# A hybrid decoder layer on one core: every SBUF tile at a new address, and a 1088-byte pitch between the token slices of x and merged

## The chip, the core and the metric

The kernel runs on one NeuronCore of one Trainium2 chip. The metric is the device time of one execution in microseconds (us). PE is TensorE, with its weight loads shown apart as PEld; DVE is VectorE, ACT is ScalarE, POOL is GpSimd and SP is SyncE, which here only issues DMAs. SBUF has 128 partitions; an address below is a byte address within each partition, the same one in all 128. PSUM takes the results of PE.

## The reference

One layer on 256 tokens of width 2048, in float32. The normalised input goes through one wide projection (12416 columns) that feeds two mixers, RWKV-7 time mixing ("a") and block-sparse attention ("b"); each result is gated, projected back to 2048 columns, the two are merged by sigmoid gates, and one output projection with a residual closes the layer:

```python
h = rms_norm(x, norm_w)
p = h @ w_in                                   # (256, 2048) @ (2048, 12416)
(p_r, p_k, p_v, z_a, p_wd, p_ad, p_q, p_kq, p_vq, z_b, g_a, g_b) = split(p)
y_a = rwkv7_mix(p_r, p_k, p_v, p_wd, p_ad, ...) * silu(z_a)      # (256, 1024)
y_b = moba_attention(p_q, p_kq, p_vq, ...) * silu(z_b)           # (256, 1024)
merged = sigmoid(g_a) * (y_a @ w_proj_rwkv) + sigmoid(g_b) * (y_b @ w_proj_moba)
out = x + merged @ w_out
```

## The kernel before

All large products run as three float32r matmuls: each operand is split into a high part and a low part (the rest), and high times high, high times low and low times high are added up in PSUM. Weights stream in from HBM in blocks of 1 MB: SP issues the load into one of two `raw` buffers, ACT writes the high part to one of three `hi` buffers (line 216), DVE writes the low part to one of three `lo` buffers (line 222). One such `hi` or `lo` tile is 128 partitions by 1024 numbers, 4096 bytes a partition.

There are two kinds of large product. `mm_fm` (line 329) keeps a 128x128 piece of the weights in PE and streams 256 tokens past it: the weights are the stationary operand, a slice of 256 tokens (1024 bytes a partition) is the moving one. `mm_tm` (lines 347 to 349) keeps 128 tokens in PE and streams 512 columns of the weights. The token operand comes from one of these tiles:

- `xh` and `xl`, the parts of x, with 16 slices of 256 tokens (one for each 128 rows of the weights, index k). Most of the input projection is `mm_fm` on them: k, r, v, the two silu gates and the two merge gates, 3504 matmuls; q, k and v of the attention are `mm_tm` on them, 576 matmuls.
- the parts of the gated mixer results, written by `y_split` into tiles that other uses have left free: `qn` (high) with `kn` (low), then `vq` with `v`, for y_b; the two halves of `bk`, then `BK` with a low part, for y_a. They hold four slices each. 768 `mm_fm` matmuls.
- `mgh` and `mgl`, the parts of merged, which take the place of `xh` and `xl` and are the stationary operand of the output projection: 336 `mm_tm` matmuls of 512 columns and 96 of 256 in the last block.

In `mm_fm` the three matmuls of one piece follow each other as high weights with high tokens, high weights with low tokens, low weights with high tokens; then come the next 128 columns, and after four of these the next k. The 128x128 pieces of a `hi` or `lo` tile are 512 bytes apart. The weights of each matmul are loaded by an instruction of their own (PEld) while the matmul before it runs.

The order of instructions on PE, ACT and DVE is fixed when the program is built, by the order in which `run_jobs` writes out loads, splits, matmuls and small pieces of the mixers' work. SBUF addresses are given by tile pools in the order in which tiles are first asked for: `T` (line 55) and `C` (line 64) ask for named tiles, and equal names share one place. Before the change, small tiles with sizes such as 396 or 4160 bytes stand among the large ones, so that large tiles begin at addresses such as 92416 or 217792.

Of the kernel before, what the change touches and what calls it, by code (L numbers as in the profile page):

```python
# [10 lines left out]
F32R = mybir.dt.float32r  # L11
# [6 lines left out]
P = 128  # L18
D = 2048
S = 256  # L20
KT = D // P
# [15 lines left out]
def tile_hybrid_block(ctx: ExitStack, tc: tile.TileContext, x, pv, wdu, wau,  # L37
                      w_in, w_pr, w_pm, w_out, out):
    nc = tc.nc
    act, dve, pool, pe, sp = nc.scalar, nc.vector, nc.gpsimd, nc.tensor, nc.sync  # L40

    cp = ctx.enter_context(tc.tile_pool(name="cp", bufs=1))
    wp = ctx.enter_context(tc.tile_pool(name="wp", bufs=2))
    sb = ctx.enter_context(tc.tile_pool(name="sb", bufs=1))
    dp = ctx.enter_context(tc.tile_pool(name="dp", bufs=1, space=bass.MemoryType.DRAM))
    pm = ctx.enter_context(tc.tile_pool(name="pm", bufs=4, space=bass.MemoryType.PSUM))
    psd = ctx.enter_context(tc.tile_pool(name="psd", bufs=4, space=bass.MemoryType.PSUM))

    cnt = [0]

    def nm(s):
        cnt[0] += 1
        return f"{s}_{cnt[0]}"

    def T(tag, shape, dt=F32, bufs=1):
        return sb.tile(shape, dt, tag=tag, name=nm(tag), bufs=bufs)

    def PSM():
        return pm.tile([P, 512], F32, tag="pm", name=nm("pm"))
# [2 lines left out]
        return psd.tile([P, 512], F32, tag="ps", name=nm("ps"))  # L62

    def C(name, shape, dt=F32):
        return cp.tile(shape, dt, tag=name, name=name)

    def f32(ap):
        return ap.bitcast(F32)


    xs = [[T(t, [P, 1024]) for t in row] for row in (("k", "cs"), ("a", "kk"))]

    def load_x(c0, c1):
# [3 lines left out]

    load_x(0, 512)
    epsr = C("epsr", [P, 1])
    pool.memset(epsr, RMS_EPS)  # L80
    ident = C("ident", [P, P])
    make_identity(nc, ident)
    PV = C("pv", [P, PV_N])
    pool.dma_start(PV, pv)
    warm = C("warm", [P, 1])
# [3 lines left out]
    m2 = C("m2", [P, 2, 64], U8)  # L89
    mq = C("mq", [P, 2, P], U8)  # L90
    mtmp = T("LL1", [P, 3, P])
    mone = T("sg", [P, P])
    pool.memset(mone, 1.0)
    for i, (step, op) in enumerate(((1, ALU.is_gt), (1, ALU.is_ge), (-1, ALU.is_ge))):
# [25 lines left out]
    X64 = T("X64", [P, 16, 64])  # L120
# [1 line left out]
        pool.memset(ap, 0.0)  # L122


    xh = C("xh", [P, KT, S], F32R)
    xl = C("xl", [P, KT, S], F32R)
    ssx = C("ssx", [P, 2, 2])
    rsx = C("rsx", [P, 2])
    rbc = C("rbc", [P, S])
# [39 lines left out]
    def normed(o, ps):  # L169
        dve.tensor_tensor(o.rearrange("p (f t) -> p f t", f=2), ps.rearrange("p (f t) -> p f t", f=2),  # L170
                          rbc2, ALU.mult)
# [186 lines left out]
    wa = C("wa", [P, S])  # L358
    xx = C("xx", [P, 4, S], F32R)
# [249 lines left out]
    yaT = C("yaT", [P, 8, S])  # L609
# [150 lines left out]
    oT = C("oT", [P, 8, S])  # L760
# [145 lines left out]
    def gate_post(key, i):  # L906
        def post(st):
            if not gates:
                for tag, n in (("LL0", 4), ("LL1", 4), ("X64", 2), ("UV", 4), ("a", 2)):
                    gt = T(tag, [P, n, 512])  # L910
                    gslots.extend(gt[:, u, :] for u in range(n))
            for j in range(2):
                gt = gslots.pop(0)
                normed(gt, st["ps"][j])
                act.activation(gt, gt, AF.Sigmoid)
                gates[key, 2 * i + j] = gt
        return post
# [15 lines left out]

    def y_split(key, src):
        for i in range(2):
            tags = ((("qn", "kn"), ("vq", "v")), (("bk",), ("BK", "ep")))["ba".index(key)][i]
            if len(tags) == 1:
                yy = T(tags[0], [P, 2, 4, S], F32R)
                yh, yl = yy[:, 0], yy[:, 1]
            else:  # L940
                yh, yl = T(tags[0], [P, 4, S], F32R), T(tags[1], [P, 4, S], F32R)
            ysp.setdefault((key, "h"), []).append(yh)
            ysp.setdefault((key, "l"), []).append(yl)
            y = src[:, 4 * i:4 * i + 4, :].rearrange("p f t -> p (f t)")
            zs = zsil[key, i].rearrange("p a t -> p (a t)")
            hv, lv = yh.rearrange("p f t -> p (f t)"), yl.rearrange("p f t -> p (f t)")
            dve.tensor_tensor(y, y, zs, ALU.mult)
            act.activation(hv, y, AF.Copy)
            yield
            dve.tensor_tensor(lv, y, f32(hv), ALU.subtract)  # L950
            yield
# [16 lines left out]
    mh_t, ml_t = [], []  # L968

    def pa_post(i):  # L970
        def post(st):
            if not mh_t:
                mh_t.append(cp.tile([P, KT, S], F32R, tag="xh", name="mgh"))
                ml_t.append(cp.tile([P, KT, S], F32R, tag="xl", name="mgl"))
            mt = T(("cs", "kk")[i % 2], [P, 2, 512])
            for j in range(2):
                m = mt[:, j, :]
                dve.tensor_tensor(m, gates["a", 2 * i + j], st["ps"][j], ALU.mult)
                dve.tensor_tensor(m, m, mrg[i, j], ALU.add)
                f0 = 4 * i + 2 * j  # L980
                hv = mh_t[0][:, f0:f0 + 2, :].rearrange("p f t -> p (f t)")
                lv = ml_t[0][:, f0:f0 + 2, :].rearrange("p f t -> p (f t)")
                act.activation(hv, m, AF.Copy)
                dve.tensor_tensor(lv, m, f32(hv), ALU.subtract)
        return post
# [54 lines left out]
    for i in range(2):  # L1040
        post = z_post("a", i, ("qkn", "lora")[i])
        if i == 1:
            post = then(post, (y_split("b", oT), None), (y_split("a", yaT), "y"))
        chunk(w_in, C_ZA + 512 * i, 512, KT, fm_x, post)
# [56 lines left out]
```

## Time and profile before

| | |
|---|---|
| time before, median of 3 runs | 836.4 us (835.27 to 838.43) |
| the profiled execution's own time | 836.63 us |
| its span, first to last instruction | 834.9 us |
| granted TensorE clock over the span | 0.998 of full speed |
| PE busy | 821.7 us, 98% of the span |
| DVE busy, ACT busy | 550.3 us (66%), 423.4 us (51%) |

The span is what the trace shows; the profiled execution's time is 1.7 us longer, and 0.2 us over the median. A busy PE is not yet a PE at its best: the recorded durations of matmuls overlap, so that the time from one start to the next is less than a duration, and it is that spacing that adds up to the span.

### The profile page before, as it was taken

The numbers are of one execution on the slowest core, as the hardware profiler recorded it, in microseconds if no ns is written. First come the engines' busy times: TensorE is split into PE (matmuls) and PEld (weight loads), VectorE is DVE, ScalarE is ACT, GpSimd is POOL, SyncE is SP. The second block draws the span as 40 slices with busy tenths as digits, with TensorE's granted clock in tenths as the row PEclk, the third lists the DMA queues.
The fourth block names the chain that finished last, engine by engine and source line by source line (L and its number), as shares of the span: only waits on it lengthen the run. The fifth ranks groups of instructions, "written<-read, shape, count | busy, mean of one in ns | idle before, by whom it ended". The sixth has DMA issues, their size and how long they took to land.

```text
span 834.9 us, 15904 instructions
## 1 busy us (share of the span) xinstructions
PE 821.7 (98%) x6770; PEld 763.3 (91%) x6770; DVE 550.3 (66%) x776; ACT 423.4 (51%) x568; POOL 28.9 (3%) x42
## 2 busy tenths in 40 slices
PE   8999999999999999999989999999999999999998
PEld 8999878899998788899989998899999999998887
DVE  5769958956569649769955578644554566665553
ACT  6785435544437576445434467654444444443332
POOL 5001200000000002000000000000000000000000
PEclk9999999999999999999999999999999999999999
DMA  8564555664434444455673324566555555556772
GB/s 305 179 199 153 178 163 165 201 177 153 150 108 142 158 152 152 156 173 187 200 220 105 106 98 151 177 202 198 186 184 193 201 186 169 201 176 203 249 231 99
DMA packets 83207, 145.78 MB, mean 175 GB/s; under 512 B 11568, under 2 KB 13872, under 8 KB 83136
## 3 DMA queue, kind: packets, MB, share of 16 engines
q1 hardware_dynamic: 71584, 138.55, 51.2%
q10 hardware_dynamic: 11520, 6.16, 2.7%
q8 instruction: 53, 0.87, 0.4%
q14 instruction: 18, 0.15, 0.1%
q0 software_dynamic: 32, 0.05, 0.0%
HBM read 141.61 MB, written 3.15 MB: 173 GB/s over the span
## 4 chain that ended last, share of the span: by engine, by line
PE 92%; ACT 3%; DVE 2%; DMA 2%; issue 1%; SPq 0%; ACTq 0%; DVEq 0%
PE pm L329 56%; PE pm L348 9%; PE pm L347 9%; PE pm L349 9%; PE ps L534 1%; PE ps L672 1%; PE ps L679 1%; ACT bk L849 1%; PE ps L878 1%; DMA td<-kk 1%; DMA cs<-td 1%; PE ps L831 1%; PE ps L696 1%; DVE lo L222 1%; ACT hi L216 1%
## 5 line engine op out<-in xcount | busy, mean ns | idle before, releaser
L222 DVE TENSOR_TENSOR lo<-raw,hi 128x1024 fp32r<-128x1024 f32 (+1 forms) x259 | 316.3, 1225 | 212.9 <-ACT hi L216 212.0
L216 ACT ACTIVATE hi<-raw 128x1024 fp32r<-128x1024 f32 (+1 forms) x259 | 272.6, 1055 | 339.1 <-PE pm L329 193.1
L329 PE MATMUL pm<-xh,hi 128*128 128x256 f32 x1168 | 326.8, 282 | 0.4 <-ACT xh L144 0.4
L329 PE MATMUL pm<-xl,hi 128*128 128x256 f32 x1168 | 324.9, 280 | 0.0
L329 PE MATMUL pm<-xh,lo 128*128 128x256 f32 x1168 | 323.9, 280 | 1.0 <-DVE lo L222 1.0
L329 PEld LDWEIGHTS pm<-xh,hi 128*128 128x128 f32 x1168 | 220.4, 190 | 3.2 <-issue 0.8
L329 PEld LDWEIGHTS pm<-xh,lo 128*128 128x128 f32 x1168 | 220.0, 190 | 2.6 <-DVE lo L222 1.4
L329 PEld LDWEIGHTS pm<-xl,hi 128*128 128x128 f32 x1168 | 220.8, 190 | 1.0 <-issue 0.3
L348 PE MATMUL pm<-lo,xh 128*128 128x512 f32 x192 | 76.3, 397 | 0.0
L349 PE MATMUL pm<-hi,xl 128*128 128x512 f32 x192 | 75.5, 393 | 0.0
L347 PE MATMUL pm<-hi,xh 128*128 128x512 f32 x192 | 74.1, 401 | 0.0
L348 PE MATMUL pm<-lo,mgh 128*128 128x512 f32 (+1 forms) x128 | 48.4, 378 | 0.0
L349 PE MATMUL pm<-hi,mgl 128*128 128x512 f32 (+1 forms) x128 | 48.0, 376 | 0.0
L347 PE MATMUL pm<-hi,mgh 128*128 128x512 f32 (+1 forms) x128 | 44.4, 377 | 0.0
L349 PEld LDWEIGHTS pm<-hi,xl 128*128 128x128 f32 x192 | 36.1, 188 | 7.8 <-issue 0.2
L348 PEld LDWEIGHTS pm<-lo,xh 128*128 128x128 f32 x192 | 36.1, 188 | 7.7 <-DVE lo L222 0.6
L347 PEld LDWEIGHTS pm<-hi,xh 128*128 128x128 f32 x192 | 35.9, 188 | 7.8 <-issue 0.5
L347 PEld LDWEIGHTS pm<-hi,mgh 128*128 128x128 f32 x128 | 24.0, 188 | 4.7
L349 PEld LDWEIGHTS pm<-hi,mgl 128*128 128x128 f32 x128 | 24.0, 188 | 4.7
L348 PEld LDWEIGHTS pm<-lo,mgh 128*128 128x128 f32 x128 | 24.0, 188 | 4.4
L566 DVE TENSOR_TENSOR tmp<-sg,kk 64x31 f32<-64x31 f32 (+15 forms) x62 | 20.6, 331 | 4.6 <-DMA sg<-gd 3.5
L329 PE MATMUL pm<-bk,hi 128*128 128x256 f32 x128 | 22.8, 281 | 0.0
(275 smaller groups left out, 990.6 us busy)
## 6 DMA issues: line engine op xcount, KB each, us to landing
raw<-in_w_in_dram SPq DMA_DIRECT2D x94, 1024.0 KB, 5.0
raw<-in_w_out_dram SPq DMA_DIRECT2D x16, 1024.0 KB, 5.6
raw<-in_w_proj_moba_dram SPq DMA_DIRECT2D x8, 1024.0 KB, 5.1
raw<-in_w_proj_rwkv_dram SPq DMA_DIRECT2D x8, 1024.0 KB, 5.2
raw<-in_w_in_dram SPq DMA_DIRECT2D x5, 512.0 KB, 6.4
k<-in_x_dram ACTq DMA_DIRECT2D x4, 256.0 KB, 5.3
r<-in_x_dram ACTq DMA_DIRECT2D x4, 256.0 KB, 4.6
k<-in_x_dram SPq DMA_DIRECT2D x2, 256.0 KB, 4.8
```

What stands on the lines that cost most here:

```text
L216: act.activation(job["hi"][:, c], job["src"][:, c], AF.Copy)
L222: dve.tensor_tensor(job["lo"][:, c], job["src"][:, c], f32(job["hi"][:, c]), ALU.subtract)
L329: pe.matmul(o, (hi, hi, lo)[ps][:, i, cs], (mh, ml, mh)[ps](k), start=(k == 0 and fi % 2 == 0 and ps == 0), stop=(k == jb["last"] and ps = ...
L347: pe.matmul(o, sh[:, k, ts], hi[:, i, cs], start=(k == 0), stop=False)
L348: pe.matmul(o, sh[:, k, ts], lo[:, i, cs], start=False, stop=False)
L349: pe.matmul(o, sl[:, k, ts], hi[:, i, cs], start=False, stop=end)
L534: pe.matmul(pss[p][:, c * P:(c + 1) * P], bk[sl, fi, c].rearrange("p a t -> p (a t)"), ar[sl, fi, c].rearrange("p a t -> p (a t)"), start= ...
L566: dve.tensor_tensor(tv, gcol.to_broadcast([64, nt, j + 1]), trow.to_broadcast([64, nt, j + 1]), ALU.mult)
L672: pe.matmul(ps[64 * p:64 * p + 64, c0 + 64 * fi:c0 + 64 * fi + 64], LL[p][:, fi, c, which, :], UV[:, c, p, fi, :], start=(fi == 0), stop=( ...
L679: pe.matmul(ps[sl, c0 + 64 * fi:c0 + 64 * fi + 64], ar[sl, fi, c, which, :], St[sl, fi, :], start=False, stop=True, skip_group_check=True)
L696: pe.matmul(ps[sl, cols], X64[sl, fi * 4 + c, :], Zs[sl, cols], start=True, stop=True)
L831: pe.matmul(pss[p][:, i * nk:(i + 1) * nk], q[rows, fi, 0:P] if u == 0 else q[rows, fi, P:S], k[rows, fi, 0:nk], start=True, stop=True)
```

## The change

The tiles get new addresses. A second pool, `sm`, takes the tiles whose size is not a multiple of 1024 bytes, so that the tiles in the other pools begin at multiples of 1024. The scratch space for software DMAs at the bottom of SBUF shrinks from 16384 to 8192 bytes. The tiles `xh`, `xl`, `mgh` and `mgl` get 16 spare numbers behind each slice, so that slices begin 1088 bytes apart, and the low ones begin 32 bytes later within their tile. Two tiles change roles: the low part that belongs to `BK` goes to `a` instead of `ep`, and two merge gates go to `ep` instead of `a`. The parts of merged are written as two pieces of 256 numbers instead of one of 512, since their slices no longer touch.

The order of the instructions on every engine, their number and what each waits for stay as they were; apart from addresses, only the names `a` and `ep` change places and the eight writes each of `mgh` and `mgl` get the other shape.

Where the operands of the large products begin, in bytes, modulo 1024 (k is the slice's index):

| tile | before | after |
|---|---|---|
| `hi`, `lo` (all six buffers; pieces at +0 and +512) | 256 | 0 |
| `xh`, `mgh`, slice k | 192 | 64k |
| `xl`, `mgl`, slice k | 192 | 352 + 64k |
| `qn` with `kn` | 640 with 704 | 0 with 0 |
| `vq` with `v` | 704 with 576 | 0 with 0 |
| `bk`, both halves | 448 with 448 | 0 with 0 |
| `BK` with its low part | 640 with 384 (`ep`) | 0 with 0 (`a`) |

```diff
@@ -42,10 +42,16 @@
     cp = ctx.enter_context(tc.tile_pool(name="cp", bufs=1))
     wp = ctx.enter_context(tc.tile_pool(name="wp", bufs=2))
     sb = ctx.enter_context(tc.tile_pool(name="sb", bufs=1))
+    sm = ctx.enter_context(tc.tile_pool(name="sm", bufs=1))
     dp = ctx.enter_context(tc.tile_pool(name="dp", bufs=1, space=bass.MemoryType.DRAM))
     pm = ctx.enter_context(tc.tile_pool(name="pm", bufs=4, space=bass.MemoryType.PSUM))
     psd = ctx.enter_context(tc.tile_pool(name="psd", bufs=4, space=bass.MemoryType.PSUM))
+
+
+    even = ("ident", "m2", "mq", "xh", "rbc", "wa", "xx", "yaT", "oT")
+    odd = ("ep", "cs", "sg", "fac", "n", "ssq", "ssk", "st", "mx", "smx")
+
     cnt = [0]
     def nm(s):
@@ -53,7 +59,7 @@
         return f"{s}_{cnt[0]}"
     def T(tag, shape, dt=F32, bufs=1):
-        return sb.tile(shape, dt, tag=tag, name=nm(tag), bufs=bufs)
+        return (sm if tag in odd else sb).tile(shape, dt, tag=tag, name=nm(tag), bufs=bufs)
     def PSM():
         return pm.tile([P, 512], F32, tag="pm", name=nm("pm"))
@@ -62,7 +68,7 @@
         return psd.tile([P, 512], F32, tag="ps", name=nm("ps"))
     def C(name, shape, dt=F32):
-        return cp.tile(shape, dt, tag=name, name=name)
+        return (cp if name in even else sm).tile(shape, dt, tag=name, name=name)
     def f32(ap):
         return ap.bitcast(F32)
@@ -122,8 +128,15 @@
         pool.memset(ap, 0.0)
-    xh = C("xh", [P, KT, S], F32R)
-    xl = C("xl", [P, KT, S], F32R)
+
+    def parts(name, tile_name):
+        off = 8 * (name == "xl")
+        pool_ = cp if name in even else sm
+        t = pool_.tile([P, off + KT * (S + 16)], F32R, tag=name, name=tile_name)
+        return t[:, off:].rearrange("p (k t) -> p k t", k=KT)[:, :, 0:S]
+
+    xh = parts("xh", "xh")
+    xl = parts("xl", "xl")
     ssx = C("ssx", [P, 2, 2])
     rsx = C("rsx", [P, 2])
     rbc = C("rbc", [P, S])
@@ -906,7 +919,7 @@
     def gate_post(key, i):
         def post(st):
             if not gates:
-                for tag, n in (("LL0", 4), ("LL1", 4), ("X64", 2), ("UV", 4), ("a", 2)):
+                for tag, n in (("LL0", 4), ("LL1", 4), ("X64", 2), ("UV", 4), ("ep", 2)):
                     gt = T(tag, [P, n, 512])
                     gslots.extend(gt[:, u, :] for u in range(n))
             for j in range(2):
@@ -933,7 +946,7 @@
     def y_split(key, src):
         for i in range(2):
-            tags = ((("qn", "kn"), ("vq", "v")), (("bk",), ("BK", "ep")))["ba".index(key)][i]
+            tags = ((("qn", "kn"), ("vq", "v")), (("bk",), ("BK", "a")))["ba".index(key)][i]
             if len(tags) == 1:
                 yy = T(tags[0], [P, 2, 4, S], F32R)
                 yh, yl = yy[:, 0], yy[:, 1]
@@ -970,16 +983,16 @@
     def pa_post(i):
         def post(st):
             if not mh_t:
-                mh_t.append(cp.tile([P, KT, S], F32R, tag="xh", name="mgh"))
-                ml_t.append(cp.tile([P, KT, S], F32R, tag="xl", name="mgl"))
+                mh_t.append(parts("xh", "mgh"))
+                ml_t.append(parts("xl", "mgl"))
             mt = T(("cs", "kk")[i % 2], [P, 2, 512])
             for j in range(2):
                 m = mt[:, j, :]
                 dve.tensor_tensor(m, gates["a", 2 * i + j], st["ps"][j], ALU.mult)
                 dve.tensor_tensor(m, m, mrg[i, j], ALU.add)
                 f0 = 4 * i + 2 * j
-                hv = mh_t[0][:, f0:f0 + 2, :].rearrange("p f t -> p (f t)")
-                lv = ml_t[0][:, f0:f0 + 2, :].rearrange("p f t -> p (f t)")
+                hv, lv = mh_t[0][:, f0:f0 + 2, :], ml_t[0][:, f0:f0 + 2, :]
+                m = m.rearrange("p (f t) -> p f t", f=2)
                 act.activation(hv, m, AF.Copy)
                 dve.tensor_tensor(lv, m, f32(hv), ALU.subtract)
         return post
@@ -1087,7 +1100,7 @@
         "w_proj_moba": a["w_proj_moba"].reshape(1024, D),
         "w_out": a["w_out"].reshape(D, D),
     }
-    nc = bacc.Bacc("TRN2", target_bir_lowering=False, num_devices=1)
+    nc = bacc.Bacc("TRN2", target_bir_lowering=False, num_devices=1, dynamic_dma_scratch_size=8192)
     arrays, args = {}, []
     for name, v in feeds.items():
         arrays[f"in_{name}_dram"] = v
```

## Rows read from the trace of the kernel before

**Rows 1.** The page: span, and each engine's busy time.

```profile
span 834.9 us, 15904 instructions
PE 821.7 (98%) x6770; PEld 763.3 (91%) x6770; DVE 550.3 (66%) x776; ACT 423.4 (51%) x568; POOL 28.9 (3%) x42
```

**Rows 2.** The page: the chain that ended last, by engine and by line.

```profile
PE 92%; ACT 3%; DVE 2%; DMA 2%; issue 1%; SPq 0%; ACTq 0%; DVEq 0%
PE pm L329 56%; PE pm L348 9%; PE pm L347 9%; PE pm L349 9%; PE ps L534 1%; PE ps L672 1%; PE ps L679 1%; ACT bk L849 1%; PE ps L878 1%; DMA td<-kk 1%; DMA cs<-td 1%; PE ps L831 1%; PE ps L696 1%; DVE lo L222 1%; ACT hi L216 1%
```

**Rows 3.** Waits of PE: us in total, times, longest.

```profile
PE ps L296 <- POOL ident masks.py:199: 2.8, 1, 2.8
...
PE pm L329 <- DVE lo L222: 1.0, 1, 1.0
```

**Rows 4.** The chain in order of time: start us, us, what.

```profile
532.05 210.94 PE pm L329 x1820
745.74 0.46 PE pm L347 x2
...
806.17 0.46 PE pm L347 x2
```

**Rows 5.** Windows: us, busy time (x instructions) by engine, granted clock, DMA share, GB/s.

```profile
31.00:49.00 18.00, 18.00 (x155) 18.00 (x155) 13.86 (x23) 13.53 (x19) 0.00 (x0) 1.00 0.63 205
70.00:80.00 10.00, 10.00 (x87) 10.00 (x86) 9.88 (x18) 4.39 (x5) 0.00 (x0) 1.00 0.41 131
...
389.00:434.00 45.00, 45.00 (x399) 45.00 (x399) 38.11 (x69) 19.23 (x21) 0.96 (x1) 1.00 0.64 202
534.00:651.00 117.00, 117.00 (x1035) 117.00 (x1034) 59.82 (x55) 53.11 (x55) 0.00 (x0) 1.00 0.60 194
652.00:742.00 90.00, 90.00 (x758) 90.00 (x757) 55.00 (x59) 38.09 (x40) 0.00 (x0) 1.00 0.57 188
```

**Rows 6.** PE groups by shape, 534 to 651 us: busy us, mean ns.

```profile
L329 PE MATMUL pm<-xl,hi 128*128 128x256 f32 x345 | 95.2, 276 | 0.0
```

**Rows 7.** PE groups by shape, 31 to 49 us.

```profile
L329 PE MATMUL pm<-xh,hi 128*128 128x256 f32 x51 | 14.3, 281 | 0.0
```

**Rows 8.** PE groups by shape, 652 to 742 us.

```profile
L329 PE MATMUL pm<-bk,hi 128*128 128x256 f32 x128 | 22.8, 281 | 0.0
L329 PE MATMUL pm<-v,hi 128*128 128x256 f32 x64 | 18.1, 282 | 0.0
L329 PE MATMUL pm<-kn,hi 128*128 128x256 f32 x63 | 18.0, 286 | 0.0
L329 PE MATMUL pm<-vq,lo 128*128 128x256 f32 x64 | 17.9, 280 | 0.0
L329 PE MATMUL pm<-vq,hi 128*128 128x256 f32 x64 | 17.9, 280 | 0.0
L329 PE MATMUL pm<-qn,lo 128*128 128x256 f32 x63 | 17.8, 283 | 0.0
L329 PE MATMUL pm<-BK,lo 128*128 128x256 f32 x62 | 17.7, 285 | 0.0
L329 PE MATMUL pm<-qn,hi 128*128 128x256 f32 x62 | 17.5, 282 | 0.0
L329 PE MATMUL pm<-BK,hi 128*128 128x256 f32 x62 | 17.4, 281 | 0.0
```

**Rows 9.** PE groups by shape, the whole span.

```profile
L329 PE MATMUL pm<-xh,hi 128*128 128x256 f32 x1168 | 326.8, 282 | 0.4 <-ACT xh L144 0.4
L348 PE MATMUL pm<-lo,xh 128*128 128x512 f32 x192 | 76.3, 397 | 0.0
L349 PE MATMUL pm<-hi,mgl 128*128 128x512 f32 x112 | 43.7, 390 | 0.0
...
L348 PE MATMUL pm<-lo,mgh 128*128 128x256 f32 x16 | 4.4, 276 | 0.0
```

**Rows 10.** ACT's writes of mgh: duration ns min/median/max, first and last start.

```profile
L983 ACT ACTIVATE mgh<-cs x4: 632/634/635, 675.7 to 722.1; 128x512 fp32r<-128x512 f32 x4
```

## The prediction, made before the changed kernel ran

> **What bounds the kernel now.** The page comes first: PE is busy 98% of a span of 834.9 us, DVE 66%, ACT 51% [rows 1], and the chain that ended last lies on PE for 92%, over half of it on line 329 alone [rows 2]. So PE decides. Does it wait? Hardly: its longest wait is 2.8 us at the start, and the large products waited once, for 1.0 us [rows 3]; from 532 us the chain is 211 us of line 329 without a break [rows 4]. What is left is how closely matmuls follow each other, and that is read from windows: length over count. The records overlap (276 ns and more each), so a window also counts about two matmuls that began before it; I take off two. At 389 to 434 us: 45,000 / 397 = 113.4 ns. At 534 to 651 us: 117,000 / 1033 = 113.3. At 31 to 49 us: 18,000 / 153 = 117.6, and at 70 to 80 us 10,000 / 85 = 117.6. At 652 to 742 us, where the tokens come from `qn` to `ep` instead of `xh` and `xl`: 90,000 / 756 = 119.0 [rows 5]. The granted clock is 1.00 in all five, the shape is the same 128x256, and PE and PEld have no gap.
>
> The mean durations say the same: 276 ns where the spacing is 113.3 [rows 6], 281 where it is 117.6 [rows 7]. A duration is thus the spacing plus 163 ns, and that gives a spacing tile by tile in the second stage, for the three matmuls of a piece: `qn` with `kn` 282, 286 and 283, so 120.7 on average; `vq` with `v` 280, 282, 280, so 117.7; `bk` 281, so 118; `BK` with `ep` up to 285, so up to 122 [rows 8]. The output projection has 512-column matmuls: from 745.74 to 806.17 us lie 22 steps of twelve matmuls, 60,430 / 264 = 228.9 ns each [rows 4].
>
> **What differs between these stages is where the operands lie.** The weight load that runs beside a matmul reads SBUF as well, so I look at the distance from the weights to the moving slice, modulo 512 (the weights step through 256 and 768 within every k, while the spacing stays at 113.3, so 512 more or less does not matter there). The table of addresses gives: `xh`, `xl` both -64; `bk` both +192; `qn` -128 with `kn` -64; `vq` -64 with `v` -192; `BK` and `ep` -128 and +128. In the last block, 256-column matmuls move `hi` at +64 from their weights, with 276 ns, so 113.3 [rows 9]. The closest spacing is seen only where high and low tokens have the same distance and it is 64 or less. Every pair with two different distances takes 117.7 or more. That is a reading of few cases: -64 itself also ran at 117.6 in the early stretches, so more than the distance plays a part.
>
> The Trainium skill ("TensorE: Matmul & The Clock Gate", Part 2, step 1) says that PE has two independent SBUF read ports and that loading the next weights takes no read bandwidth from the running matmul. By that rule the distance could not matter, and the sum would be nothing. The rows for 534 and 652 us speak against it, 113.3 against 119.0 ns with no wait in either; it lives on as the rival of no change.
>
> **The change part by part.** No instruction is added, removed or moved, so every term is a spacing.
>
> *x as the moving operand*, 3504 matmuls (three groups of 1168 [rows 9]). Their present mean: in the clean windows 238 at 117.6 and 1430 at 113.3, so about 114 ns; I take that for all, the rest being cut up by other work. After the change the distance is 64k for the high part and 64k - 160 for the low one: it takes all eight multiples of 64 as k runs, and high and low never agree. Bounds: 113.3 (everything as close as seen) and 120.7 (as `qn` with `kn`). I take the row whose two distances are most nearly as far apart, `vq` with `v` at 128: 117.7. That is 3504 x 3.7 ns = +13.0 us; by the bounds -2.5 and +23.5.
>
> *The mixers' parts as the moving operand*, 768 matmuls at 119.0 now. All now begin at multiples of 1024, high and low alike, with distance 0, which lies between -64 and +64, both seen at 113.3. I take that: 768 x -5.7 = -4.4 us. The other bound is `bk`'s 118, equal distances too: -0.8.
>
> *512-column matmuls*, 576 in the input projection and 336 in the output projection. Their distance spreads over the multiples of 64 as well. The groups run from 390 to 397 ns, so 227 to 234 in spacing [rows 9] (the 397 holds interruptions by other work); I take 0, by the bounds 912 x -1.9 = -1.7 and 912 x +5.1 = +4.7 us. The last 96 of 256 columns are 1% of the work: nothing.
>
> *Everything else* I cost at nothing: ACT's writes of `mgh` take 633 ns now [rows 10] and become two-piece writes of the same 512 numbers; they and DVE's work lie beside PE, which is busy for all 90 us of that stage while ACT and DVE are busy 38 and 55 us [rows 5]. Were this cover gone, eight writes slowed by half would cost 8 x 0.3 = 2.5 us. Weight loads land at other addresses; the large products' only wait for a split was 1.0 us [rows 3], so loads have room. The exchange of `a` and `ep` brings no new wait. The smaller DMA scratch serves POOL's one DMA at the start.
>
> Sum: +13.0 - 4.4 = +8.6 us on the profiled execution's 836.6 us, 1.7 us of which lie outside the span: 845.2. That execution was 0.2 over the median, so 845.0 on the scale of 836.4.
>
> **Rivals.**
>
> *Faster: every stretch reaches 113.3.* If what slowed the pairs of the 652 us stage was a beginning at odd offsets rather than two different distances, the mixers' stage and the early 117.6 stretches both close up, and x loses nothing: -2.5 - 4.4 - 1.7 = -8.6, so 828. For it: after a disturbance x mostly fell back to 113.3, with 1430 of the 1668 clean matmuls. Against it: no pair with two distances has shown it. It decides once x stays at 114.0 or less; at 115.3 the two terms cancel.
>
> *No change.* Either addresses do not matter, and the stages differ by something the trace doesn't name: 836.4. Or the k whose high part lies within 64 (three of eight) stay at 113.3 and the rest take 117.7: a mean of 116.0, +7.0 - 4.4 = +2.6, so 839.
>
> *Below 113.3.* The new 32-byte shift of the low part is the one address that is no multiple of 64, and no row has such an operand; it could set the two reads apart for good. No clean row shows a 256-column spacing under 113.3, so the rows give it no price beyond the 828 above. The Trainium skill (the same page, "Back-to-back issue gap") gives N/2.4 + 2.5 ns, 109.2 for 256 columns and 215.8 for 512; by it, as an estimate, all three terms together would be -36 us, and the trace's 113.3 and 228.9 do not agree with it so far.
>
> **How the numbers follow.** The forecast, x slower than the mixers' part gains: 0.46, at 845.0, its own range 841 to 854. Every stretch at 113.3: 0.27. Below that: 0.05. No change in both forms: 0.22. A change within 0.5%, 4.2 us, can't be told from none here. So faster 0.32, same 0.22, slower 0.46. The range for 8 in 10 leaves out the bottom of the fast cases and the top of the slow one (the bound of 120.7 on x reaches 863 with all upper bounds): 826 to 854.
>
> **What would show it.** In the new profile the window over the input projection's last 120 us gives x alone: 117 to 118 ns, and 281 ns recorded, is the forecast, 113.3 and 276 the fast rival; and if k matters, neighbouring slices differ in a steady pattern of eight. The stage after it should fall from 119.0 to 113.3, 4.4 us shorter whatever x does. The output projection's twelve matmuls should again take 2.75 us. The prediction is wrong if x keeps its 113.3, if distance 0 is worse than the pairs of now (both streams beginning at the same place), or if waits of PE appear in the list.

## The result, and the profile after

The changed kernel takes 847.96 us (847.23 to 849.19, 4 runs) against 836.53 us in the same comparison: a ratio of 1.0136 (95% interval 1.0113 to 1.0159, as with every ratio below), so 11.4 us slower where 8.6 were forecast. The profiled execution's span is 846.4 us, 11.5 more than before. The head of the new page:

```profile
span 846.4 us, 15904 instructions
PE 834.4 (99%) x6770; PEld 774.2 (91%) x6770; DVE 551.9 (65%) x776; ACT 423.0 (50%) x568; POOL 29.0 (3%) x42
...
PE 92%; ACT 3%; DVE 2%; DMA 2%; issue 1%; SPq 0%; ACTq 0%; DVEq 0%
```

Against [rows 1, 2] the counts are the same, ACT and DVE are as busy as they were, and PE is busy 12.7 us longer. The difference is all PE, and the waits of PE are no longer than before (lines have moved by 13: 329 is now 342, 347 to 349 are 360 to 362):

```profile
PE ps L309 <- POOL ident masks.py:199: 2.8, 1, 2.8
PE ps L608 <- DMA cs<-td: 1.9, 1, 1.9
PE ps L876 <- ACT hi L229: 1.5, 1, 1.5
PE pm L342 <- DVE lo L235: 1.0, 1, 1.0
```

So it is spacing. The windows of the changed kernel over an early stretch of x, the late stretch of x and the stage of the mixers' parts, in the columns of [rows 5]:

```profile
37.00:51.00 14.00, 14.00 (x121) 14.00 (x121) 10.85 (x19) 12.71 (x18) 0.00 (x0) 1.00 0.53 176
...
543.00:660.00 117.00, 117.00 (x998) 117.00 (x997) 57.66 (x52) 50.35 (x53) 0.00 (x0) 1.00 0.58 189
662.00:752.00 90.00, 90.00 (x752) 90.00 (x751) 54.79 (x58) 37.47 (x39) 0.00 (x0) 1.00 0.57 187
```

With two taken off each count: 14,000 / 119 = 117.6 ns early; 117,000 / 996 = 117.5 in the late stretch, which was 113.3; 90,000 / 750 = 120.0 with the mixers' parts, which was 119.0. The clock is 1.00 throughout. The chain in order of time gives the output projection:

```profile
537.07 215.97 PE pm L342 x1820
755.81 0.46 PE pm L360 x2
...
817.11 0.47 PE pm L360 x2
```

The same 1820 matmuls take 215.97 us instead of 210.94 [rows 4], and 22 steps of twelve matmuls take 61.30 us: 232.2 ns each, which was 228.9. All three kinds of large product got slower.

### The profile page after: what moved, and what is told of

It is laid out like the page before. It is cut to its first block, busy times and chain, and to the rows that moved or that the text cites. A ratio compares the mean times of both kernels' runs of the same rounds, so it can differ in the third digit from the quotient of the medians.

```text
span 846.4 us, 15904 instructions
## 1 busy us (share of the span) xinstructions
PE 834.4 (99%) x6770; PEld 774.2 (91%) x6770; DVE 551.9 (65%) x776; ACT 423.0 (50%) x568; POOL 29.0 (3%) x42
## 4 chain that ended last, share of the span: by engine, by line
PE 92%; ACT 3%; DVE 2%; DMA 2%; issue 1%; SPq 0%; ACTq 0%; DVEq 0%
PE pm L342 56%; PE pm L360 9%; PE pm L361 9%; PE pm L362 9%; PE ps L547 1%; PE ps L685 1%; PE ps L692 1%; ACT bk L862 1%; DMA cs<-td 1%; PE ps L891 1%; DMA td<-kk 1%; PE ps L844 1%; PE ps L709 1%; DVE lo L235 1%; DMA raw<-in_w_in_dram 1%
## 5 line engine op out<-in xcount | busy, mean ns | idle before, releaser
L342 PE MATMUL pm<-xh,lo 128*128 128x256 f32 x1168 | 327.6, 283 | 1.0 <-DVE lo L235 1.0
L342 PE MATMUL pm<-xl,hi 128*128 128x256 f32 x1168 | 328.2, 282 | 0.0
```

Source lines behind the costliest of these rows:

```text
L342: pe.matmul(o, (hi, hi, lo)[ps][:, i, cs], (mh, ml, mh)[ps](k), start=(k == 0 and fi % 2 == 0 and ps == 0), stop=(k == jb["last"] and ps = ...
```

## The experiments

The theory at this point: the spacing follows from the distance between the moving slice and the weights that are being loaded. The first four kernels set that distance. All keep the order of instructions on PE, ACT and DVE (pads add two small writes on POOL at the start); spacings below are from windows over the late stretch of x and over the mixers' stage, worked out as above.

**Equal distances for high and low.** `xl` joins the tiles at multiples of 1024, and the 32 bytes go:

```diff
-    even = ("ident", "m2", "mq", "xh", "rbc", "wa", "xx", "yaT", "oT")
+    even = ("ident", "m2", "mq", "xh", "xl", "rbc", "wa", "xx", "yaT", "oT")
...
-        off = 8 * (name == "xl")
+        off = {"xh": 0, "xl": 0}[name]
```

> The changed kernel with the low parts' 32-byte shift gone and xl at a multiple of 1024: slices still 1088 bytes apart, but high and low tokens of x now have the same distance from the weights, 64k. Theory 'distance' (the spacing of matmuls follows from the distance between the moving slice and the weights, modulo 512, and equal distances of -64 and +64 are good): slices with 64k equal to 64 or 448 modulo 512 run at 113.3 ns, the others at 117 to 120, x on average near 117.5, total 846 to 849 us. Rival 'unequal pair' (x lost its 113.3 only because high and low no longer agree): x at 113.3 but for k = 0 and 8, total about 834 us. Rival 'shift of 32 bytes' (only the odd address of the low part costs): as the unequal pair, and the slices do not differ from each other.

Measured: 847.85 us, ratio 1.0131 (1.0081 to 1.0182), and 110,000 / 936 = 117.5 ns for x:

```profile
545.00:655.00 110.00, 110.00 (x938) 110.00 (x937) 54.32 (x49) 47.72 (x51) 0.00 (x0) 1.00 0.57 185
```

The 32-byte shift and the pair that doesn't agree are not what cost x its 113.3. The start times of single matmuls, put beside the program's slices, give the spacing by slice over the late stretch, some 60 matmuls a slice:

| distance 64k, modulo 512 | 0 | 64 | 128 | 192 | 256 | 320 | 384 | 448 |
|---|---|---|---|---|---|---|---|---|
| mean spacing, ns | 118.4 | 118.1 | 118.6 | 115.4 | 118.4 | 118.1 | 118.6 | 115.4 |

It repeats after 256 bytes, not 512. The slices at 192 and at 448, which is -64 modulo 512, are the close ones: the first five spacings of each lie between 114 and 124 ns and the other seven at 113 to 114, so a mean over twelve is not yet the steady spacing.

**All at distance 0.** In addition slices are 1024 bytes apart (`KT * S` in place of `KT * (S + 16)`).

> The changed kernel with slices 1024 bytes apart again and xl at a multiple of 1024: every moving operand at distance 0 from the weights. Theory 'distance': x takes what the mixers' parts take at distance 0, 120.0 ns, so 3504 x 2.5 ns on top of the changed kernel, 855 to 858 us. Rival 'pitch' (1088 instead of 1024 is what cost x): x back at 113.3 ns, 834 us, while the mixers' stage stays at 120. Rival 'stage' (the mixers' stage is slower for a reason that is no address): the same 834 us.

Measured: 851.82 us, ratio 1.018 (1.0128 to 1.0232). Both stages of this kernel:

```profile
543.00:662.00 119.00, 119.00 (x994) 119.00 (x993) 58.13 (x52) 51.20 (x54) 0.00 (x0) 1.00 0.56 182
664.00:754.00 90.00, 90.00 (x752) 90.00 (x752) 55.40 (x59) 38.30 (x40) 0.00 (x0) 1.00 0.56 181
```

119,000 / 992 and 90,000 / 750: 120.0 ns in both. So x at distance 0 behaves as the mixers' parts do there, the stage has no slowness of its own, and the pitch of 1024 does not bring 113.3 back by itself. The changed addresses are also those at which ACT and DVE read and write, so accesses of other engines are a rival. The start times speak against it: from 545 to 655 us of this kernel all 917 spacings are 120 ns, the 122 during which ACT and DVE both rest as well as the 119 during which both work. Where all distances are -64 (the next kernel, 545 to 645 us) the mean is 113.3 to 113.4 in either case. The total is below the 855 to 858 expected, in good part because 512-column matmuls are faster at distance 0: this kernel's groups of the output projection are at 389 and 390 ns, where the changed kernel has 393 to 396:

```profile
L361 PE MATMUL pm<-lo,mgh 128*128 128x512 f32 x112 | 43.7, 390 | 0.0
L362 PE MATMUL pm<-hi,mgl 128*128 128x512 f32 x112 | 43.6, 389 | 0.0
```

**All at -64, and all at +64.** The weights get a pad ahead (64 or 960 bytes, and the rest of 1024 behind them), all else as at distance 0:

```diff
+    w0 = ctx.enter_context(tc.tile_pool(name="w0", bufs=1))
     wp = ctx.enter_context(tc.tile_pool(name="wp", bufs=2))
+    w1 = ctx.enter_context(tc.tile_pool(name="w1", bufs=1))
...
+    pads = [q.tile([P, n], F32, tag=t, name=t) for q, n, t in ((w0, 16, "pad0"), (w1, 240, "pad1"))]
```

> As the kernel with all at distance 0, but the weights 64 bytes later: every moving slice of the 256-column products at -64 from its weights, as x was before the change. Theory 'distance': x and the mixers' parts both at 113.3 ns, the stage after the gates 5.7 ns a matmul faster than before the change (4.4 us), total 829 to 833 us. Rival 'stage': x at 113.3, the mixers' stage still at 118 to 120, total 836 us. Rival 'multiples of 1024' (a moving operand that begins at a multiple of 1024 is slow wherever the weights are): x and the mixers at 120, 855 us.

> As the kernel with all at distance 0, but the weights 64 bytes earlier (960 modulo 1024): every moving slice of the 256-column products at +64 from its weights, which only the 256-column matmuls of the last block had before the change. Theory 'distance': 113.3 ns for x and the mixers' parts, 829 to 833 us. Rival 'multiples of 1024': 120 ns, 855 us. A spacing between the two would say that +64 is not like -64, and that the reading of the last block's 96 matmuls was too wide.

At -64: 834.72 us, ratio 0.9972 (0.9946 to 0.9998), over the 829 to 833 expected. An early stretch, the late one and the mixers' stage:

```profile
34.00:43.00 9.00, 9.00 (x82) 9.00 (x81) 7.40 (x15) 5.15 (x9) 0.00 (x0) 1.00 0.44 137
534.00:650.00 116.00, 116.00 (x1026) 116.00 (x1025) 58.96 (x54) 52.97 (x55) 0.00 (x0) 1.00 0.60 194
653.00:736.00 83.00, 83.00 (x735) 83.00 (x734) 52.89 (x57) 36.48 (x38) 0.00 (x0) 1.00 0.60 195
```

116,000 / 1024 = 113.3 for x and 83,000 / 733 = 113.2 for the mixers' parts. 64 bytes between the weights and everything else are worth 6.7 ns a matmul, 120.0 against 113.3. "Stage" and "multiples of 1024" fall.

At +64: 845.85 us, ratio 1.0101 (1.0052 to 1.0151), not the expected 829 to 833. Two windows over x in this one execution:

```profile
397.00:432.00 35.00, 35.00 (x311) 35.00 (x310) 32.28 (x59) 16.08 (x17) 0.96 (x1) 1.00 0.59 191
543.00:655.00 112.00, 112.00 (x954) 112.00 (x953) 55.41 (x50) 48.05 (x51) 0.00 (x0) 1.00 0.57 188
```

35,000 / 309 = 113.3 and 112,000 / 952 = 117.6, with the same addresses and the same clock. The mixers' stage at +64, 661 to 750 us, takes 89,000 / 756 = 117.7. So a distance can have two spacings, and distance alone does not say all; what picks one is open.

**The two parts of the change, each alone on the kernel before.** The first moves only the weight tiles from 256 to 0 modulo 1024 (pads of 768 and 256 bytes around their pool); the second only sets the slices of x and merged 1088 bytes apart. Both need the smaller DMA scratch, and the second writes the parts of merged in two pieces, as the change does. The second, cut:

```diff
-    xh = C("xh", [P, KT, S], F32R)
-    xl = C("xl", [P, KT, S], F32R)
+    def parts(name, tile_name):
+        t = cp.tile([P, KT * (S + 16)], F32R, tag=name, name=tile_name)
+        return t.rearrange("p (k t) -> p k t", k=KT)[:, :, 0:S]
+
+    xh = parts("xh", "xh")
+    xl = parts("xl", "xl")
```

> One part of the change alone, on the kernel before: the raw, hi and lo tiles go from 256 to 0 modulo 1024, every other tile stays where it was modulo 1024 (the DMA scratch shrinks to make room). Theory 'period 256': every distance moves by 256, so nothing changes: x at 113.3 ns in the late stretch, the mixers' stage near 119, 836 us. Rival 'multiples of 1024' (weights there are bad, or good, in themselves): x away from 113.3, up to 120 ns, so up to 856 us. Rival 'period 512 or 1024': x at distance 192 there takes 117 to 118, 847 us.

> The other part alone, on the kernel before: slices of x and merged 1088 bytes apart, weights still at 256 modulo 1024, the mixers' tiles where they were. x's distance is then -64 + 64k, high and low alike. Theory 'distance': x loses its 113.3 as in the changed kernel, 117.5 to 117.7 ns on average, +10 to +12 us, while the mixers' stage stays near 119: 846 to 848 us, so the pitch is most of the change. Rival 'both parts together': less than half of it, 840 us or under.

Weights only: 835.48 us, ratio 0.9986 (0.9966 to 1.0005), no change; x and the mixers' stage of this kernel are

```profile
534.00:650.00 116.00, 116.00 (x1026) 116.00 (x1025) 59.13 (x54) 52.81 (x55) 0.00 (x0) 1.00 0.61 196
655.00:741.00 86.00, 86.00 (x725) 86.00 (x724) 52.85 (x57) 35.64 (x37) 0.00 (x0) 1.00 0.58 185
```

or 113.3 and 118.9 ns, as before the change. All distances moved by 256 and nothing happened: period 256 holds, and multiples of 1024 are neither good nor bad for weights. By that period `bk` in the kernel before lies at -64 like x (192 is -64 modulo 256), both halves alike. Yet it ran at 281 ns [rows 8], so at 118, in the same execution in which x ran at 113.3: the two spacings of one distance were there before the change. Pitch only: 848.37 us, ratio 1.0122 (1.0091 to 1.0153):

```profile
545.00:655.00 110.00, 110.00 (x938) 110.00 (x937) 54.36 (x49) 47.75 (x51) 0.00 (x0) 1.00 0.58 188
```

That is 117.5 ns. The pitch of 1088 bytes alone gives the whole slowdown.

**A map in steps of 16 bytes.** Weights at 0, slices of x 1040 bytes apart (`S + 4`), high and low alike, so that the sixteen slices pass once through the period.

> A map: the changed kernel with the weights at multiples of 1024 and the slices of xh and xl 1040 bytes apart, equal for high and low, so that slice k has distance 16k. The kernel with slices 1088 apart showed slices 256 bytes of distance apart alike (0 as 256, 64 as 320, 128 as 384, 192 as 448). Theory 'period 256': these sixteen slices walk once through it; 0 near 118 to 120, 64 and 128 near 118, 192 at 113 to 116, and the values between say how wide the good place is. Rival 'multiples of 64': distances that are no multiple of 64 behave unlike any seen so far, below 113.3 if the two reads then never meet. x's mean in the late stretch: 116 to 118 by the first, anything by the second.

Measured: 848.87 us in one run, and 110,000 / 936 = 117.5 ns for x on average:

```profile
545.00:655.00 110.00, 110.00 (x938) 110.00 (x937) 54.31 (x50) 47.84 (x50) 0.00 (x0) 1.00 0.59 191
```

By slice, some 60 matmuls each:

| distance | 0 | 16 | 32 | 48 | 64 | 80 | 96 | 112 |
|---|---|---|---|---|---|---|---|---|
| ns | 119.0 | 119.3 | 116.3 | 118.3 | 113.4 | 119.1 | 120.0 | 113.3 |
| distance | 128 | 144 | 160 | 176 | 192 | 208 | 224 | 240 |
| ns | 117.8 | 119.0 | 117.3 | 118.9 | 114.7 | 118.8 | 118.5 | 117.2 |

The good places are narrow: 64, 112 and 192, each between neighbours 16 bytes off at 117 to 120. No slice has a mean below 113.3. But each value is that of twelve matmuls that follow a slice at another distance, not of a stretch that stays: 64 has 113.4 here, where the kernel that stays at +64 had 117.6 in its late stretch. From this kernel's timeline, the first matmul of each of five slices in a row, with twelve matmuls to a slice:

```profile
599.59 0.28 PE L342 MATMUL pm<-xh,hi 128*128 128x256 f32 x1
...
600.95 0.28 PE L342 MATMUL pm<-xh,hi 128*128 128x256 f32 x1
...
602.38 0.28 PE L342 MATMUL pm<-xh,hi 128*128 128x256 f32 x1
...
603.82 0.28 PE L342 MATMUL pm<-xh,hi 128*128 128x256 f32 x1
...
605.18 0.28 PE L342 MATMUL pm<-xh,hi 128*128 128x256 f32 x1
```

The first four are the slices at 64, 80, 96 and 112: 1.36, 1.43, 1.44 and 1.36 us for twelve.

**Staying at 112, and going back and forth between 64 and 192.** The first has the weights at 928 and slices at 16, 1024 apart (the mixers' parts then lie at 96); the second has weights at 960 and slices 1152 apart.

> Slices 1024 bytes apart, every slice of x at distance 112 from its weights (weights at 928, slices at 16 modulo 1024), the mixers' parts at 96. In the map with steps of 16 bytes, distance 112 ran at 113.3 and 96 at 120.0. Theory 'distance alone': x at 113.3 ns in the late stretch and the mixers' parts at 120; 834 to 838 us. Rival 'state': two spacings are possible at such a distance and what ran before picks one (as -64 showed both 113.3 and 117.6 before the change), so that a kernel that stays at 112 can sit at 117 to 118 for long stretches; up to 848 us.

> Slices 1152 bytes apart, weights at 960 modulo 1024: x's distance alternates between 64 (even k) and 192 (odd k), modulo 256. A constant 64 ran at 117.8 ns, a constant 192 at 113.3, and 64 within the map of 16-byte steps at 113.4. Theory 'distance alone': even slices 117.8, odd ones 113.3, a mean of 115.5. Rival 'state': both distances can run at 113.3, and once the close spacing is reached at 192 it is kept at 64, so all slices at 113.3 after a while; or both at 117.8 if the slow one is kept.

At 112: 113,000 / 998 = 113.2 ns for x, and two early windows, 36 to 44 and 56 to 64 us, count 73 matmuls each, 8,000 / 71 = 112.7: close from early on. Still 842.7 us, ratio 1.0079 (1.0058 to 1.0101), more than the 834 to 838 expected. By start times, all of x took 420.2 us, against 420.6 before the change, so 112 is no gain over -64; the mixers' parts at 96 take 88,000 / 734 = 119.9, 0.8 us more than before; and the 912 512-column matmuls, where the weights are the moving operand and the distance is turned round, take 3.5 us more, near 233 ns in the output projection. The window of the late stretch:

```profile
539.00:652.00 113.00, 113.00 (x1000) 113.00 (x999) 57.48 (x53) 50.60 (x53) 0.00 (x0) 1.00 0.60 196
```

Back and forth: 844.77 us in one run, and x at 110,000 / 950 = 115.8. Its late window:

```profile
545.00:655.00 110.00, 110.00 (x952) 110.00 (x951) 54.19 (x50) 48.88 (x51) 0.00 (x0) 1.00 0.58 191
```

Its timeline has a slice at 64 and one at 192:

```profile
601.03 0.28 PE L347 MATMUL pm<-xh,hi 128*128 128x256 f32 x1
...
602.44 0.28 PE L347 MATMUL pm<-xh,hi 128*128 128x256 f32 x1
...
603.81 0.28 PE L347 MATMUL pm<-xh,hi 128*128 128x256 f32 x1
```

1.41 us for twelve, then 1.37: the spacing changes with each slice, as distance alone would have it, and the close spacing is not carried over to 64. The rival of states, in the form that one spacing is kept over both distances, fails here. Distance alone does not fit all runs either: the kernel at a constant 64 showed two spacings, and 64 in the map ran at 113.4.

**The kernel at -64 once more, in more runs.**

> The kernel with every moving slice at -64 from its weights once more, in more rounds, since its first interval (0.9946 to 0.9998) nearly reaches 1. The mixers' stage is 768 matmuls at 113.3 instead of 119.0 ns, 4.4 us less; the first 160 us may run at 113.3 or 117.6 from one kernel to the next. Theory: ratio 0.993 to 0.997, 830 to 834 us on the scale of 836. Rival: the two states of -64 make whole executions differ by more than the gain, so that the ratio is 0.997 to 1.001.

Measured: 835.53 us, ratio 0.9995 (0.9977 to 1.0013): the rival, no difference from before. Its early stretch and its mixers' stage:

```profile
34.00:43.00 9.00, 9.00 (x79) 9.00 (x78) 7.06 (x14) 4.87 (x8) 0.00 (x0) 1.00 0.46 142
655.00:741.00 86.00, 86.00 (x761) 86.00 (x760) 54.46 (x59) 38.27 (x40) 0.00 (x0) 1.00 0.59 196
```

The mixers' stage is again at 86,000 / 759 = 113.3. But early it is 9,000 / 77 = 116.9 where the same program's other execution had 9,000 / 80 = 112.5. The spacing at -64 is thus not fixed by the program: two executions of it took different ones over the same stretch. The spans of the two profiled executions are 830.5 and 833.2 us, both under the 834.9 of before, while the timed runs do not confirm a gain. Whether unprofiled executions also take the slow spacing in the mixers' stage can't be seen; that stays open.

## Why the prediction came out as it did

The direction was right, and so was the mechanism in its outline: no instruction moves, PE is bound by the spacing of its matmuls, and the spacing depends on the distance between the moving slice and the weights. Why it does, whether the two reads get in each other's way or something else, no run shows. At distance 0 and at -64 the same matmuls in the same order run at 120.0 and 113.3 ns. The Trainium skill ("TensorE: Matmul & The Clock Gate", Part 2, step 1) says that loading the next weights takes no read bandwidth from the running matmul. As the prediction read it, the distance could then not matter, and these traces do not agree.

*x as the moving operand, +13.0 forecast.* The spacing forecast, 117.7, was 117.5. The price was too high. The groups of the whole span, which hold the cut-up stretches too, rise by less: high times high from 282 [rows 9] to 284, the other two from 280 to 282 and 283:

```profile
L342 PE MATMUL pm<-xh,hi 128*128 128x256 f32 x1168 | 329.4, 284 | 0.2 <-ACT xh L157 0.2
...
L342 PE MATMUL pm<-xl,hi 128*128 128x256 f32 x1168 | 328.2, 282 | 0.0
L342 PE MATMUL pm<-xh,lo 128*128 128x256 f32 x1168 | 327.6, 283 | 1.0 <-DVE lo L235 1.0
```

That is 1168 x (2 + 2 + 3) ns = 8.2 us; from start to start all 3504 rose from 420.6 to 429.1 us, 8.5. The step "about 114 ns; I take that for all" was mis-sized: where other work cuts x up, it was not that close before, and lost less. Between neighbours with nothing else between them the mean was 115.2 ns from 100 to 389 us and 114.5 over the span, and became 117.7. The reason given was wrong in one part: high and low that disagree are not needed. Equal distances at a pitch of 1088, or the pitch alone on the old kernel, cost the same; it is that the distance walks through places of which most are slow. That the forecast of 117.7 came from `vq` with `v`, a pair chosen for its two unequal distances, and still hit 117.5 is thus luck in part.

*The mixers' parts, -4.4 forecast.* This step failed. "Distance 0 lies between -64 and +64, both seen at 113.3" took a smooth curve for granted. The map shows narrow places with slow ones 16 bytes beside them; distance 0 is slow, 120.0, and the stage lost 768 x 1.0 = 0.8 us. Modulo 512 was the wrong period too: the experiments show 256.

*512-column matmuls, 0 forecast, bounds -1.7 and +4.7.* In the output projection 228.9 became 232.2: 336 x 3.3 = 1.1 us; in the input projection the three groups rose by 1 to 2 ns, about 1 us; the last block's 96 rose from 276 to about 281 ns, 0.5 us. The value lay inside the bounds, but it is a term, not nothing. (The range of 390 to 397 ns behind the upper bound left out one group of the input projection, which had 401 before the change.)

Together 8.2 + 0.8 + 1.1 + 1.0 + 0.5 = 11.6 us against 11.5 of span. The total of the forecast came near because the high price of x and the gain that did not come, 4.8 and 5.2 us, nearly cancelled, which is luck; what is left of the difference between 8.6 and 11.5 is mostly the 512-column matmuls and the last block, 2.6 us together. Of the rivals, "every stretch reaches 113.3" needed distances that the change does not give, and for "below 113.3" no slice of the map speaks. "Distance 0 worse than the pairs of now", named among the signs of being wrong, came true: 120.0 against 119.0. The costs set at nothing held: ACT's and DVE's totals and PE's waits stayed.

## What to carry to other kernels

Where PE is busy all the time and waits for nothing, divide a window by its count: a spacing that differs between stages of equal shape is worth looking for in the operands' addresses, and it can be worth 1 to 2% of the span without any change of order. A pitch that is a multiple of the period (here 256 bytes) keeps the moving operand's slices at one distance from the weights, where another pitch walks through many. One distance is not better by itself: all at 0 took 851.8 us, the walk 848, all at -64 835. So try that one distance on the chip; good ones here had slow neighbours 16 bytes away. A spacing read from one stretch of one execution may be one of two, so look at several stretches, and let many timed runs, not one profile, decide on a gain under 1%.

## What was not expected of the hardware

- The spacing of 256-column float32r matmuls depends on the distance of moving operand and weights in SBUF with a period of 256 bytes: 113.3 ns at the best places, 117 to 120 at most others; a shift of all weights by 64 bytes took it from 120.0 to 113.3.
- The same distance can run at two spacings: 113.3 and 117.6 in two stretches of one execution at +64, and 112.5 and 116.9 over the same stretch in two executions of one program at -64. The same execution of the kernel before had x at -64 at 113.3 and `bk` at -64 at 118. What picks between them is open. An alternation of 64 and 192 changed with each slice, 1.41 and 1.37 us for twelve, so there the close spacing is not carried from slice to slice.
- None of sixteen distances, 16 bytes apart, had a mean below 113.3 ns. By start times the spacing does not depend on whether ACT and DVE work beside PE: 120 ns each for 917 matmuls at distance 0.
- 512-column matmuls with the weights as the moving operand rank the distances otherwise: 226.7 ns at 0, where the others are slowest (a step of twelve takes 2.72 us in the chain of that kernel), 228.9 before the change and near 233 with x at 112.
